# A decoder layer's output product: half of its weight sums made earlier and kept in DRAM

## The chip, the core and the metric

The kernel runs on one core of a Trainium2 chip. The metric is the device time of one execution in microseconds (us); the number that is predicted is the median of several runs.

## What is computed

One layer of a decoder over 512 tokens of width 2048, in float32: a norm, one combined projection `h @ w_in`, two groups of attention heads, the output product, and a gated feed-forward part. The change touches the output product alone:

```python
h = rms_norm(x, norm1_g[l])
proj = h @ w_in[l]
...
mix = jnp.concatenate([out_a.astype(x.dtype), out_b.astype(x.dtype)], axis=-1)
x = x + mix @ w_out[l]
h2 = rms_norm(x, norm2_g[l])
x = x + (jax.nn.silu(h2 @ w_gate[l]) * (h2 @ w_up[l])) @ w_down[l]
```

`w_out` is 2048 x 2048; its first half is its columns 0 to 1023.

## The kernel before

Every large product is cut into **pairs**: 1024 columns of a weight matrix, taken as two halves of 512 columns (`w1`, `w2`), against 512 rows of tokens. The reduction of 2048 is cut into four groups `g` of two 256-row halves. Within a group the 2 x 2 block product is done with seven products in place of eight (a Winograd form): three of them use a quarter of the weights as it is (`SINGLE`: P1 takes quarter a, P3 takes d, P2 takes c), four use a sum of quarters (`SUMS_OF`: P5 needs b - a, P6 needs d less that, P7 needs d - b, P4 needs c less the P6 sum). Seven products of four groups are 28 **items** of a pair, in the order P1 (items 0 to 3), P5 (4 to 7), P6 (8 to 11), P3 (12 to 15), P7 (16 to 19), P2 (20 to 23), P4 (24 to 27).

For an item `stream` (L318) issues four things. `total` (L325) calls `Pair.source`: the quarter is loaded with `load_quarter` (L219, DMA at L222, 512 KB, one tile of `wpool`, which has 12), and where a sum is due VectorE makes it in place at L256. `first_part` (L329) rounds the source to the high part `wh` on ScalarE (L331), `second_part` (L333) takes the low part `wl` on VectorE (L335). Then TensorE does 8 matmuls with `wh` and 4 with `wl` (L361). `wh` and `wl` have two tiles each, so an item can be prepared about two items ahead. TensorE, VectorE and ScalarE each take their instructions strictly in the order in which the scheduler put them, and so does the queue of SyncE (SP), which issues all loads and stores: a DMA that waits holds every DMA behind it.

Beside the items runs **background** work, one piece at a time after the `wh` matmuls of an item (`step`, L502): attention heads, transposes, and the activation side of the next product. `split` (L172) makes the high and low parts of an activation operand (ScalarE L174, VectorE L175).

The first pair (queries and keys of the gated heads) is issued by a table of its own (`first_pair`). `stream` does the others. In what follows they are counted as in the change: the **second pair** makes two value halves (`va1`, `va0`), the **third** `qb0`, `kb0`, the **fourth** `vb1`, `vb0`, the fifth `qb1`, `kb1`, the sixth the output gate. The **seventh** is the first half of the output product (`pair(opm, rows_mix, ocol(0), ocol(512), final_out(0), ...)`, L1416), the eighth its second half; eleven pairs of the gate and up products and six of the down product follow. In the seventh pair the background makes the operands S1, S2, S4, A12 and A22 of that same product (`late_jobs`, L1225: sums on VectorE at L1234, L1236, L1238 and a `split` each).

The second pair also carries `gates` (L768) and `bias_tables` (L598); the latter ends in `rep_d` (L618), one DMA of 2560 KB from DRAM to DRAM. The third and fourth carry the gated heads (`gla_head`, L823). `rpool` has four tiles of 128 x 512 floats; they hold activations in the first pair, and from the end of the fourth on the dilated heads and the sums of `late_jobs` use them. `final_proj` (L1084) stores each projection to DRAM (L1092).

## Time and profile before

| | |
|---|---|
| median of 3 runs | 1980.36 us (1979.09 to 1982.37) |
| the profiled execution, its own time | 1983.93 us |
| its span | 1982.1 us |
| TensorE busy | 1933.1 us (98%) |
| VectorE busy | 1652.7 us (83%) |
| ScalarE busy | 1095.9 us (55%) |
| GpSimd busy | 60.1 us (3%) |
| DMA moved | 360.44 MB, mean 182 GB/s |

The times in the trace are counted from the span's start. PE is TensorE's matmuls, PEld its weight loads, DVE is VectorE, ACT is ScalarE, POOL is GpSimd, and SPq is SyncE's queue, which issues the DMAs. An arrow in a group of instructions (`wl<-wa,wh`) reads "writes wl from wa and wh", with buffer numbers left out. The second pair stands from 105.0 to 184.1 us, the third to 277.3, the fourth to 363.5, and the seventh from 574.4 to 654.1. What ended an idle time stands behind `<-`. Busy times of PE are modelled, so the spacing of its starts says more than its durations.

### The profile page before, as it was taken

How to read it: one execution, taken by the hardware profiler on the slowest of the kernel's cores; microseconds unless marked ns; L12 is line 12 of the kernel's file. 1: busy time of each engine (PE TensorE's matmuls, PEld its weight loads, DVE VectorE, ACT ScalarE, POOL GpSimd, SP SyncE). 2: the span in 40 equal slices, each digit the busy share in tenths (PEclk: the TensorE clock that was granted, in tenths of full speed). 3: DMA queues.
4: the chain of work that ended last, by engine and by line, in shares of the span. 5: the costliest groups of instructions: out<-in, count | busy, mean ns of one | idle time of the engine just before them, and what ended most of it. 6: DMA issues, size and time to landing. Idle time of an engine off the chain costs nothing.

```text
span 1982.1 us, 25779 instructions
## 1 busy us (share of the span) xinstructions
PE 1933.1 (98%) x9226; PEld 1671.1 (84%) x9226; DVE 1652.7 (83%) x1850; ACT 1095.9 (55%) x1600; POOL 60.1 (3%) x81
## 2 busy tenths in 40 slices
PE   7999999999999999999999999999999999999998
PEld 6888888888787777888888888888888888888887
DVE  7997787768689789878878878878879989989987
ACT  6664564566676666545445445445446646546443
POOL 0000231011000000000000000000000000000000
PEclk9999999999999999999999999999999999999999
DMA  8357455454575685654554554554555855955762
GB/s 276 118 171 251 132 182 169 141 162 151 182 232 187 222 267 170 180 160 133 181 164 134 176 164 128 174 166 128 174 161 164 292 195 187 310 182 172 249 212 75
DMA packets 237113, 360.44 MB, mean 182 GB/s; under 512 B 18247, under 2 KB 96784, under 8 KB 236985
## 3 DMA queue, kind: packets, MB, share of 16 engines
q1 hardware_dynamic: 236776, 358.72, 57.1%
q8 instruction: 72, 1.18, 0.2%
q14 instruction: 57, 0.46, 0.1%
q10 hardware_dynamic: 208, 0.08, 0.0%
HBM read 296.59 MB, written 64.51 MB: 182 GB/s over the span
## 4 chain that ended last, share of the span: by engine, by line
PE 75%; DVE 8%; DMA 5%; issue 3%; ACT 2%; POOL 1%; SPq 0%; DVEq 0%; ACTq 0%; POOLq 0%
PE acc L361 70%; DVE wl L335 3%; DVE wa L256 2%; PE bank L1112 1%; DVE AS L175 1%; DMA xn_d<-PT 1%; PE bank L1009 1%; ACT wh L331 1%; PE bank L977 1%; DMA T<-x_d 0%; DMA top<-mix_d 0%; PE bank L1002 0%; DMA r<-xn_d 0%; DMA wc<-in_w_in 0%; DVE wb L256 0%
## 5 line engine op out<-in xcount | busy, mean ns | idle before, releaser
L361 PE MATMUL acc<-wh,AS 128*128 128x512 f32 x3008 | 712.7, 380 | 2.0 <-ACT wh L331 2.0
L361 PEld LDWEIGHTS acc<-wh,AS 128*128 128x128 f32 x3008 | 568.3, 189 | 84.8 <-ACT wh L331 4.0
L331 ACT CAST wh<-wa 128x1024 fp32r<-128x1024 f32 x376 | 393.3, 1048 | 401.3 <-PE acc L361 378.9
L361 PE MATMUL acc<-wh,AA 128*128 128x512 f32 x2256 | 537.1, 381 | 9.6 <-ACT wh L331 9.6
L335 DVE TENSOR_TENSOR wl<-wa,wh 128x1024 fp32r<-128x1024 f32 x376 | 456.9, 1219 | 85.0 <-ACT wh L331 49.6
L361 PEld LDWEIGHTS acc<-wh,AA 128*128 128x128 f32 x2256 | 427.4, 190 | 72.8 <-ACT wh L331 11.9
L361 PE MATMUL acc<-wl,AS 128*128 128x512 f32 x1504 | 396.6, 386 | 10.1 <-DVE wl L335 9.9
L361 PEld LDWEIGHTS acc<-wl,AS 128*128 128x128 f32 x1504 | 279.2, 189 | 64.0 <-DVE wl L335 23.1
L361 PE MATMUL acc<-wl,AA 128*128 128x512 f32 x1128 | 297.1, 386 | 2.8 <-DVE wl L335 2.7
L361 PEld LDWEIGHTS acc<-wl,AA 128*128 128x128 f32 x1128 | 210.5, 190 | 35.8 <-DVE wl L335 6.3
L331 ACT CAST wh<-wb 128x1024 fp32r<-128x1024 f32 x94 | 98.5, 1049 | 120.0 <-PE acc L361 112.9
L331 ACT CAST wh<-wc 128x1024 fp32r<-128x1024 f32 x94 | 98.3, 1047 | 112.9 <-PE acc L361 104.8
L331 ACT CAST wh<-wd 128x1024 fp32r<-128x1024 f32 x94 | 98.5, 1048 | 105.6 <-PE acc L361 101.5
L256 DVE TENSOR_TENSOR wa<-wc,wa 128x1024 f32<-128x1024 f32 x94 | 114.6, 1222 | 45.6 <-DMA wc<-in_w_gate 29.0
L335 DVE TENSOR_TENSOR wl<-wd,wh 128x1024 fp32r<-128x1024 f32 x94 | 114.4, 1220 | 38.5 <-ACT wh L331 29.5
L335 DVE TENSOR_TENSOR wl<-wc,wh 128x1024 fp32r<-128x1024 f32 x94 | 114.6, 1220 | 35.0 <-ACT wh L331 34.2
L335 DVE TENSOR_TENSOR wl<-wb,wh 128x1024 fp32r<-128x1024 f32 x94 | 113.6, 1217 | 4.9 <-ACT wh L331 4.4
L256 DVE TENSOR_TENSOR wb<-wd,wb 128x1024 f32<-128x1024 f32 x94 | 114.5, 1218 | 1.1 <-DMA wd<-in_w_in 0.7
L256 DVE TENSOR_TENSOR wa<-wb,wa 128x1024 f32<-128x1024 f32 x94 | 113.6, 1219 | 0.8
L256 DVE TENSOR_TENSOR wa<-wd,wa 128x1024 f32<-128x1024 f32 x94 | 112.8, 1218 | 0.1
L298 DVE SCALAR_TENSOR_TENSOR seed<-acc,rs,seed 128x512 f32<-128x512 f32 x96 | 70.4, 746 | 23.2 <-PE acc L361 23.2
L282 ACT ACTIVATE seed<-acc,rs 128x512 f32<-128x512 f32 x96 | 60.7, 682 | 1.2 <-PE acc L361 1.0
(289 smaller groups left out, 1368.7 us busy)
## 6 DMA issues: line engine op xcount, KB each, us to landing
wa<-in_w_gate SPq DMA_DIRECT2D x44, 512.0 KB, 4.2
wb<-in_w_up SPq DMA_DIRECT2D x44, 512.0 KB, 4.3
wd<-in_w_up SPq DMA_DIRECT2D x44, 512.0 KB, 4.4
wc<-in_w_gate SPq DMA_DIRECT2D x44, 512.0 KB, 3.7
wc<-in_w_in SPq DMA_DIRECT2D x28, 512.0 KB, 3.7
wa<-in_w_in SPq DMA_DIRECT2D x24, 512.0 KB, 5.1
wb<-in_w_in SPq DMA_DIRECT2D x24, 512.0 KB, 6.0
wd<-in_w_in SPq DMA_DIRECT2D x24, 512.0 KB, 5.4
```

Source lines behind the costliest of these rows:

```text
L175: nc.vector.tensor_tensor(a[:, :, 1, :], src, a[:, :, 0, :].bitcast(F32), op=ALU.subtract)
L256: nc.vector.tensor_tensor(src, self.quarter(one, g), src, op=ALU.subtract)
L282: nc.scalar.activation(halves(t), unfolded(src[m]), AF.Copy, scale=self.scale(half, m))
L298: nc.vector.scalar_tensor_tensor(halves(seed[m]), unfolded(src[m]), self.scale(half, m), halves(seed[m]), op0=ALU.mult, op1=ALU.add,)
L331: nc.scalar.copy(high[k], sources[k])
L335: nc.vector.tensor_tensor(low[k], sources.pop(k), high[k].bitcast(F32), op=ALU.subtract)
L361: nc.tensor.matmul(p.dst[prod][m], a[:, jj, hl, m * P : (m + 1) * P], folded(w[:, jj, :]), start=fresh and g == 0 and len(terms) == 2 and ...
L977: nc.tensor.matmul(lp[:, :n], qh[:, b * P : (b + 1) * P], kh[:, :n], start=True, stop=True)
L1009: nc.tensor.matmul(op, vh[:, k, :], lgs[b][:, k * P : (k + 1) * P], start=(k == 0), stop=(k == b))
L1112: nc.tensor.transpose(bk[:, jj, m * P : (m + 1) * P], tiles[m][:, f : f + P], ident)
```

## The change

The 16 sums of quarters that the seventh pair makes on VectorE are made elsewhere. A new generator `weight_sums` loads, for each group and each 128-row half of a quarter, the four quarters a, b, d, c of `w_out` into the four tiles of `rpool` (128 x 512, 256 KB each), makes the four sums there with four VectorE instructions, and stores each to a DRAM tensor (`P5_g_d`, `P7_g_d`, `P6_g_d`, `P4_g_d`). There are eight such rounds: 32 loads, 32 sums, 32 stores. `side(2)` takes one step of the generator at every second item of the second, third and fourth pair. In the seventh pair `source` loads a stored sum (512 KB) where it used to make it, and the quarters a, d and c are loaded for P1, P3 and P2 alone, and released after use; b is not loaded there any more.

```diff
         def source(self, prod, g):
             if prod in SINGLE:
-                return self.quarter(SINGLE[prod], g)
+                t = self.quarter(SINGLE[prod], g)
+                if self.sums:
+                    self.q.pop((SINGLE[prod], g))
+                return t
+            if self.sums:
+                t = wpool.tile([P, 2, 512], F32, name=nm("ws"), tag="w")
+                load(t, self.sums[prod, g])
+                return t
             one, two = SUMS_OF[prod]
...
+    def weight_sums(rows, w1, w2, sums):
+        tt = nc.vector.tensor_tensor
+        def fetch(g, j):
+            res = []
+            for name in "abdc":
+                r0 = rows[g][0 if name in "ab" else 1] + P * j
+                t = rpool.tile([P, 2, 256], F32, name=nm("r"), tag="r").rearrange(
+                    "p a b -> p (a b)")
+                load(t, (w1 if name in "ac" else w2)[r0 : r0 + P, :])
+                res.append(t)
+            return res
+        for g in range(4):
+            for j in range(2):
+                a, b, d, c = fetch(g, j)
+                yield
+                yield
+                tt(a, b, a, op=ALU.subtract)
+                tt(b, d, b, op=ALU.subtract)
+                yield
+                tt(d, d, a, op=ALU.subtract)
+                tt(c, c, d, op=ALU.subtract)
+                for prod, t in (("P5", a), ("P7", b), ("P6", d), ("P4", c)):
+                    store(sums[prod, g][:, j, :], t)
+                yield
...
+    def side(units):
+        count = [0]
+        def go():
+            count[0] += 1
+            if aside and count[0] % units == 0:
+                try:
+                    next(aside[0])
+                except StopIteration:
+                    aside.pop(0)
+        return go
+    def both(*fns):
+        return lambda: [fn() for fn in fns]
...
+    aside.append(weight_sums(rows_mix, ocol(0), ocol(512), out_sums))
+    beside = side(2)
-    pair(opx, rows_in, col(1536), col(1024), final_proj("va1", "va0"), rate((22, 1), (6, 0.6)),
+    pair(opx, rows_in, col(1536), col(1024), final_proj("va1", "va0"),
+         both(rate((22, 1), (6, 0.6)), beside),
          row_scale, before=lambda: background.extend([gates(), bias_tables()]))
     flow = rate((84, 0.55))
-    pair(opx, rows_in, col(3088), col(4112), final_proj("qb0", "kb0"), flow, row_scale)
-    pair(opx, rows_in, col(5648), col(5136), final_proj("vb1", "vb0"), flow, row_scale)
+    flowing = both(flow, beside)
+    pair(opx, rows_in, col(3088), col(4112), final_proj("qb0", "kb0"), flowing, row_scale)
+    pair(opx, rows_in, col(5648), col(5136), final_proj("vb1", "vb0"), flowing, row_scale)
...
-    pair(opm, rows_mix, ocol(0), ocol(512), final_out(0), paced([1] * 28),
+    pair(opm, rows_mix, ocol(0), ocol(512), final_out(0), paced([1] * 28), sums=out_sums,
```

The scheduler sets the order on each engine, and three places of it are shown. In the changed kernel line 335 of before is L371, line 256 is L264, line 1092 is L1146 and line 618 is L672; L345 to L349 are the new sums, L336 their loads, L351 their stores.

The first place is VectorE in the seventh pair, from the end of P5 into P6 (`wa<-wd,wa` are the sums for P6, `AS` the splits of S1, `r` the sums of `late_jobs`). Before:

```order
L1236 TENSOR_TENSOR r_5300<-r_5300,qT_5370 128x512
L256 TENSOR_TENSOR wa_5200<-wd_5463,wa_5200 128x1024
L175 TENSOR_TENSOR AS_1058_5454<-r_5300,AS_1058_5454 128x2x256
L335 TENSOR_TENSOR wl_5466<-wa_5314,wh_5461 128x1024
L1236 TENSOR_TENSOR r_5326<-r_5326,kT_5395 128x512
L256 TENSOR_TENSOR wa_5228<-wd_5488,wa_5228 128x1024
L175 TENSOR_TENSOR AS_1063_5479<-r_5326,AS_1063_5479 128x2x256
L335 TENSOR_TENSOR wl_5491<-wa_5200,wh_5486 128x1024
```

The same stretch with the change (`ws` is a stored sum):

```order
L371 TENSOR_TENSOR wl_5579<-ws_5551,wh_5575 128x1024
L175 TENSOR_TENSOR AS_1084_5568<-r_5470,AS_1084_5568 128x2x256
L175 TENSOR_TENSOR AS_1090_5594<-r_5444,AS_1090_5594 128x2x256
L1290 TENSOR_TENSOR r_5470<-r_5470,kT_5537 128x512
L371 TENSOR_TENSOR wl_5605<-ws_5577,wh_5601 128x1024
L175 TENSOR_TENSOR AS_1095_5618<-r_5470,AS_1095_5618 128x2x256
L1292 TENSOR_TENSOR r_5384<-v_5565,r_5384 128x512
L371 TENSOR_TENSOR wl_5629<-ws_5603,wh_5625 128x1024
```

The instruction of 1024 columns between two `wl` is gone, and more of the `late_jobs` work stands ahead of a given item.

The second place is SP's queue in the second pair, around `rep_d`; `wc` are the quarters for its P2 items, `va` the stores of a projection. Before, two of the four `wc` loads stand there:

```order
L222 DMA wc_1607<-in_w_in 128x2x512
L618 DMA rep_d<-bias_d 1024x1x640
L1092 DMA va_177<-seed_1471 128x512
L1092 DMA va_177<-seed_1489 128x512
L222 DMA wc_1626<-in_w_in 128x2x512
```

With the change:

```order
L351 DMA P_0_d<-r_1458 128x512
L672 DMA rep_d<-bias_d 1024x1x640
L351 DMA P_0_d<-r_1460 128x512
L1146 DMA va_177<-seed_1511 128x512
L1146 DMA va_177<-seed_1529 128x512
L336 DMA r_1613<-in_w_out 128x512
L336 DMA r_1615<-in_w_out 128x512
L336 DMA r_1617<-in_w_out 128x512
L222 DMA wc_1663<-in_w_in 128x2x512
L222 DMA wc_1682<-in_w_in 128x2x512
```

The third and fourth `wc` loads now stand behind `rep_d`, two stores of a projection and three loads into `r` tiles, whose last one needs the tile of the store just behind `rep_d`.

The third place is VectorE in the P2 items of the second pair (items 20 to 23). Before:

```order
L335 TENSOR_TENSOR wl_1609<-wc_1587,wh_1605 128x1024
L298 SCALAR_TENSOR_TENSOR seed_1410<-acc_1147,rs_103,seed_1410 128x512
L335 TENSOR_TENSOR wl_1628<-wc_1607,wh_1624 128x1024
L256 TENSOR_TENSOR wa_1187<-wc_1626,wa_1187 128x1024
L335 TENSOR_TENSOR wl_1659<-wc_1626,wh_1656 128x1024
```

With the change:

```order
L371 TENSOR_TENSOR wl_1665<-wc_1643,wh_1661 128x1024
L306 SCALAR_TENSOR_TENSOR seed_1442<-acc_1163,rs_103,seed_1442 128x512
L345 TENSOR_TENSOR r_1611<-r_1613,r_1611 128x512
L346 TENSOR_TENSOR r_1613<-r_1615,r_1613 128x512
L348 TENSOR_TENSOR r_1615<-r_1615,r_1611 128x512
L349 TENSOR_TENSOR r_1617<-r_1617,r_1615 128x512
L264 TENSOR_TENSOR wa_1166<-wc_1663,wa_1166 128x1024
L371 TENSOR_TENSOR wl_1684<-wc_1663,wh_1680 128x1024
```

A whole round of four new sums and one sum of the pair itself stand between the second and the third `wl` of P2. In the whole order 16 of the 32 new sums stand ahead of the third pair's first `wl` and 16 in the third pair; none is left for the fourth.

## Rows read from the trace of the kernel before

**Rows 1.** The page, part 1: busy us (share of the span) xinstructions of each engine.

```profile
PE 1933.1 (98%) x9226; PEld 1671.1 (84%) x9226; DVE 1652.7 (83%) x1850; ACT 1095.9 (55%) x1600; POOL 60.1 (3%) x81
```

**Rows 2.** The page, part 4: the chain that ended last, by engine.

```profile
PE 75%; DVE 8%; DMA 5%; issue 3%; ACT 2%; POOL 1%; SPq 0%; DVEq 0%; ACTq 0%; POOLq 0%
```

**Rows 3.** Busy time of each engine in stretches; the first line names the columns.

```profile
core 0: us, PE busy (x) PEld busy (x) DVE busy (x) ACT busy (x) POOL busy (x), PEclk, DMA share, GB/s
105.00:184.00 79.00, 77.85 (x363) 66.28 (x362) 66.57 (x70) 41.29 (x51) 0.39 (x2) 1.00 0.61 202
184.00:277.30 93.30, 93.01 (x474) 79.92 (x473) 73.67 (x96) 50.21 (x111) 17.03 (x27) 1.00 0.58 178
574.40:654.10 79.70, 76.21 (x354) 64.52 (x353) 78.39 (x91) 51.16 (x76) 0.00 (x0) 1.00 0.60 198
900.00:975.00 75.00, 74.38 (x353) 64.83 (x352) 60.10 (x59) 36.95 (x43) 0.00 (x0) 1.00 0.51 158
165.00:184.00 19.00, 19.00 (x96) 16.44 (x95) 12.72 (x16) 8.30 (x10) 0.39 (x2) 1.00 0.87 283
```

**Rows 4.** L361, seventh pair: what TensorE sat idle for: us, times.

```profile
  DVE wl L335: 8.5, 10
```

**Rows 5.** Timeline of PE, seventh pair: starts of the wh matmuls of single items.

```profile
592.21 1.89 PE L361 MATMUL acc<-wh,AS 128*128 128x512 f32 x8
...
609.43 1.89 PE L361 MATMUL acc<-wh,AS 128*128 128x512 f32 x8
...
612.02 1.89 PE L361 MATMUL acc<-wh,AS 128*128 128x512 f32 x8
...
614.62 1.89 PE L361 MATMUL acc<-wh,AS 128*128 128x512 f32 x8
...
630.15 1.89 PE L361 MATMUL acc<-wh,AS 128*128 128x512 f32 x8
...
633.33 1.89 PE L361 MATMUL acc<-wh,AA 128*128 128x512 f32 x8
```

**Rows 6.** Timeline of DVE, seventh pair: one item's instructions: start us, us.

```profile
597.91 0.68 DVE L1236 TENSOR_TENSOR r<-r,kT 128x512 f32<-128x512 f32 x1
598.51 1.22 DVE L256 TENSOR_TENSOR wa<-wd,wa 128x1024 f32<-128x1024 f32 x1
599.65 0.68 DVE L175 TENSOR_TENSOR AS<-r,AS 128x512 fp32r<-128x512 f32 x1
600.25 1.22 DVE L335 TENSOR_TENSOR wl<-wa,wh 128x1024 fp32r<-128x1024 f32 x1
601.38 0.68 DVE L1238 TENSOR_TENSOR r<-v,r 128x512 f32<-128x512 f32 x1
```

**Rows 7.** L361, second and third pair: what TensorE sat idle for: us, times.

```profile
  DVE wl L335: 4.1, 6
```

**Rows 8.** Timeline of SP's DMA issues, second pair: start us, us.

```profile
145.55 0.72 SPq L618 DMA_DIRECT2D rep_d<-bias_d  x1
151.79 2.11 SPq L1092 DMA_DIRECT2D va<-seed  x2
153.95 0.43 SPq L222 DMA_DIRECT2D wc<-in_w_in  x1
...
165.16 1.49 SPq L222 DMA_DIRECT2D wa<-in_w_in  x3
```

**Rows 9.** DMA issues of the second pair: xcount, KB each, median us to landing.

```profile
wc<-in_w_in SPq DMA_DIRECT2D x4, 512.0 KB, 3.6
...
wb<-in_w_in SPq DMA_DIRECT2D x4, 512.0 KB, 7.5
va<-seed SPq DMA_DIRECT2D x6, 256.0 KB, 9.5
```

**Rows 10.** Timelines of ACT and PE, second pair, item 22: its cast and its first matmuls.

```profile
162.70 1.05 ACT L331 CAST wh<-wc 128x1024 fp32r<-128x1024 f32 x1 [1.54 <-PE acc L361]
...
165.96 1.89 PE L361 MATMUL acc<-wh,AA 128*128 128x512 f32 x8
```

11 lines of the change are left out of this document (8 added, 3 removed).

## The prediction

> **What bounds the kernel now.** First the busy shares, then the chain that ended last. TensorE is busy for 98% of the span, with VectorE next at 83% [rows 1], and the chain stands 75% on TensorE and 8% on VectorE [rows 2]. So a change can win only where TensorE waits, and it loses where it makes TensorE wait. Third, the stretches [rows 3]: a quiet pair of the feed-forward part takes 75.0 us with 60.1 us of VectorE work. The seventh pair takes 79.7 us with 78.4 us of VectorE work: there VectorE is full. Fourth, what TensorE waits for there: VectorE's `wl`, ten times, 8.5 us with matmuls and weight loads counted both [rows 4]. The starts of the items give the loss without double counting. An undisturbed item takes 614.62 - 612.02 = 2.60 us. The five from 592.21 to 609.43 take 17.22 us where 5 x 2.60 = 13.0 us would do, and the one from 630.15 to 633.33 takes 3.18 us [rows 5]. That is 4.2 + 0.6 = 4.8 us. The comparison with the quiet pair gives 79.7 - 75.0 = 4.7 us [rows 3]. Fifth, VectorE inside one slow item [rows 6]: sum, weight sum, split and `wl` start at 597.91, 598.51, 599.65 and 600.25, and the next item's first at 601.38, so one item costs VectorE 3.47 us. Its two sizes cost 0.60 us (512 columns) and 1.14 us (1024), start to start.
>
> **What is removed.** The seventh pair loses 16 weight sums, 16 x 1.14 = 18.2 us of VectorE [rows 6]. Without its weight sum the slow item needs 3.47 - 1.14 = 2.33 us, under the 2.60 us of TensorE. More work of the background comes into some items in its place (first place in the order: two splits and a sum before one `wl`, 3 x 0.60 + 1.14 = 2.94 us), but others get lighter, and `wl` can be two items ahead. So I take the whole 4.8 us as gained. Bounds: half of it (2.4 us), if the background's own loads now hold VectorE; 5.5 us, if also waits on ScalarE in that pair shrink.
>
> **What is added, VectorE.** 32 sums of 512 columns, 32 x 0.60 = 19.2 us, 16 in the second and 16 in the third pair: 9.6 us each. They are covered by VectorE's idle time there, 79.0 - 66.6 = 12.4 us and 93.3 - 73.7 = 19.6 us [rows 3]. The cover is not even. Where four new sums stand together before one `wl` (third place in the order), that item needs 0.67 (a `seed`, taken a little over the 512-column sum) + 4 x 0.60 + 2 x 1.14 = 5.4 us against 2.6 us, and the lead of two items just about pays for it. I take 0.5 us for such places. Bounds: 2 us, and a gain of 1 us, since TensorE already waits 4.1 us for `wl` in these two pairs [rows 7] and the new order also moves work out of some of those waits.
> [...] The rows have two starts of 0.60 us in place of one of 1.14 us [rows 6], 16 x 0.06 = 1 us in all, and I go by the rows.
>
> **What is added, DMA in the second and third pair.** 32 loads and 32 stores of 256 KB, 16.8 MB, half of it in each pair. The second pair moved 202 GB/s at a share of 0.61, which is 331 GB/s at full share; with 8.4 MB over 79 us it would move 308 GB/s [rows 3]. Its last 19 us are at 283 GB/s and a share of 0.87 already [rows 3]. So transfers queue there, and what counts is who stands behind whom on SP. The worst place I find is the second place in the order. The third `wc` quarter now stands behind a load into an `r` tile that must wait for the store just behind `rep_d` to land. `rep_d` was issued at 145.55 and the first store after it at 151.79 [rows 8]; such stores took 9.5 us to land [rows 9]. So that tile comes free at about 161, the `wc` load goes out at about 162 and lands 3.6 us later at best [rows 9], at 165.6. Its cast ran at 162.70 with TensorE's item at 165.96 [rows 10]; the latest harmless start is 165.96 - 1.05 = 164.9. So it is 0.7 us late at best, and 4.6 us if it takes the 7.5 us that the `wb` loads took [rows 9]. Three loads leave just ahead of it, so I take 1.5 us, nearer to the 3.6 us row because those loads are small. Lower bound 0.
> Other waits that are added cost nothing by their leads. New stores that wait on SP for a VectorE sum hold the third pair's `wa` loads, which went out from 165.16 on [rows 8] and are first needed near 183, 18 us later. `gates`, `rep_d` and the heads shift by one or two VectorE instructions and are read a pair later. GpSimd's queue is not touched.
>
> **What is added, DMA in the seventh pair.** 28 loads of 512 KB where there were 16: 6.3 MB more over 79.7 us, 79 GB/s on top of 198 at a share of 0.60 [rows 3], so some 0.84. Each weight tile is now used by one item and free again, so the twelve tiles run further ahead of TensorE than before. I cost this at nothing; if that cover fails it is the 2.4 us of the lower bound above.
>
> **Sum.** -4.8 + 0.5 + 1.5 = -2.8 us against the profiled execution's own 1983.93 us, that is 1981.1 us. That execution lies 3.6 us above the median of the runs, so in terms of the median 1980.36 - 2.8 = 1977.6 us. About 0.2%, 4 us, is what a measurement of this kernel can tell from no change.
>
> **The rivals.**
> *Clean gain.* The loads find room, the late `wc` quarter is no later than its slack, and the crowded places fall into existing waits: -4.8 to -5.5 us, 1975.3 us. For it: VectorE has 32 us idle in the two pairs [rows 3]. Against it: the SP order above.
> [...]
> *Half a gain.* In the seventh pair the loads of `late_jobs` stand on SP between loads of weights, each of which now waits for an item's `wl`. If they come late, splits hold the casts and 2.4 us are left of the gain: -2.4 + 2.0 = -0.4 us, 1980.0 us. Against it: `late_jobs` fetches three pieces ahead.
> *Slower: SP's queue in the second and third pair.* The wait of a load for a store decides, from the point where a store takes the 9.5 us of the `va` row [rows 9] everywhere and not only behind `rep_d`. Then the `wc` quarter is 4.6 us late. The third pair's `wa` quarters, behind four stores that wait for sums near 168 and four loads that wait for these to land, go out at about 180 where they went at 165.16 [rows 8], land 7.5 us later [rows 9] and hold the pair's start by some 4 us (187.5 against a need near 183). With 0.5 us for crowding: 4.6 + 4 + 0.5 - 4.8 = +4.3 us, 1984.7 us. For it: 0.87 of the DMA engines busy at that place [rows 3]. Against it: the `wc` loads landed in 3.6 us.
>
> **How the numbers follow.** Forecast 42%, clean gain 25%, half a gain 15%, slower 18%. Faster by over 0.2%: the clean gain and the lowest part of the forecast, 0.30. Slower by over 0.2%: the last rival and a little of the half gain, 0.20. Within 0.2%: 0.50. The range goes from the clean gain with the repeat spread of 1.3 us below the median (1974.0) to the slow rival's value with a little over it (1985.5); the forecast's own range, 1976 to 1980, is the sum with the `wc` term between 0 and 3 us.
>
> **What would show it.** Right: in the seventh pair VectorE's busy time falls by some 18 us, TensorE's waits for `wl` fall from 8.5 to under 2 us, and the pair takes about 75 us; in the second pair a cast of `wc` waits for its DMA by one to two us near item 22, and TensorE after it; the third pair is as long as before. Wrong: if the seventh pair stays over 77 us, its limit was not the weight sums; if the second and third pair together grow by over 5 us, or TensorE waits for `wa` at the third pair's start, the SP term was too small; if they do not grow at all, it was imagined.

## The result, and the profile after

Six runs of the changed kernel have a median of 1988.03 us (1985.34 to 1997.26), six of the kernel before 1980.57 us (1979.09 to 1982.37). The ratio is 1.0034 with an interval of 1.0020 to 1.0048: the change costs 4 to 9.5 us. The prediction of 1977.6 us was wrong, and so was its range, which ended at 1985.5 us.

The two profiled executions show less than that. The one of before took 1983.93 us, above all its timed runs; the one of after took 1985.34 us, the lowest of its six. So the traces tell where time went, and the runs tell how much. Busy time first (page, part 1, kernel after):

```profile
PE 1931.9 (97%) x9226; PEld 1670.8 (84%) x9226; DVE 1654.8 (83%) x1866; ACT 1095.4 (55%) x1600; POOL 67.6 (3%) x81
```

Against [rows 1] nothing of note moved: VectorE has 2.1 us more work in all, and the totals hide two changes that nearly cancel. The stretches show them. These are the second, third and seventh pair of after (columns as in [rows 3]):

```profile
105.00:191.00 86.00, 80.68 (x363) 67.76 (x363) 75.68 (x86) 41.27 (x51) 0.45 (x2) 0.96 0.74 236
191.00:290.60 99.60, 94.37 (x476) 79.83 (x475) 84.01 (x112) 50.61 (x112) 22.87 (x27) 1.00 0.88 283
...
584.60:660.90 76.30, 74.80 (x354) 65.08 (x353) 62.69 (x76) 50.77 (x76) 0.00 (x0) 1.00 0.92 302
```

The seventh pair is 3.4 us shorter, with 15.7 us less of VectorE's work [rows 3]; TensorE's waits for `wl`, 8.5 us in [rows 4], are gone, and this is all that is left there (what L397's matmuls and weight loads sat idle for, after, seventh pair):

```profile
  ACT wh L367: 3.3, 2
```

But the second pair is 7.0 us longer and the third 6.0 us. Lengths of pairs are taken here and below from the first `wh` matmul of a pair to that of the next. All else is 8.2 us shorter by these two traces, 3.6 us of it in the sixth pair and 4.8 us in the eighth. The sixth pair takes 109.6 to 114.2 us in the kernels of this study, whatever was changed elsewhere, so its part can't be told from chance. Of the eighth pair's 4.8 us, 3.3 us stand at its items 1 to 4 and belong to the gain: in 15 of the 17 kernels whose seventh pair makes none or half of its sums these items are 2.7 to 3.3 us shorter than before (in hole 1.2 us shorter, in skip_second 0.5 us longer), and in cost_alone, which makes them all, 0.3 us longer. Its last item takes from 2.2 us less to 0.8 us more in these kernels without any pattern, so its 1.4 us are not told from chance either.

**The second pair.** SP's queue (after, timeline of its issues; start us, us):

```profile
145.87 0.72 SPq L672 DMA_DIRECT2D rep_d<-bias_d  x1
148.30 3.38 SPq L351 DMA_DIRECT2D P_d<-r  x1
152.37 2.11 SPq L1146 DMA_DIRECT2D va<-seed  x2
154.53 8.65 SPq L336 DMA_DIRECT2D r<-in_w_out  x3
163.22 0.94 SPq L222 DMA_DIRECT2D wc<-in_w_in  x2
...
181.29 2.06 SPq L222 DMA_DIRECT2D wa<-in_w_in  x4
```

A store of a sum leaves just behind `rep_d`. Three loads into `r` tiles follow at 154.53, and their issue takes 8.65 us: the last waits for that store to land. The two `wc` quarters stand behind it and go out at 163.22; before, the later of them went at 153.95 [rows 8]. In the second and third pair such waits add up to this (after, waits of SP's queue: us, times, longest):

```profile
SPq L336 <- DMA P_d<-r: 17.2, 11, 7.3
```

ScalarE's cast for item 22 and TensorE's matmuls of items 21 to 23 show what it costs (after, timelines of ACT and PE; compare [rows 10]):

```profile
169.71 1.04 ACT L367 CAST wh<-wc 128x1024 fp32r<-128x1024 f32 x1 [8.41 <-DMA wc<-in_w_in]
```

```profile
165.22 1.03 PE L397 MATMUL acc<-wl,AA 128*128 128x512 f32 x4
170.81 3.78 PE L397 MATMUL acc<-wh,AA 128*128 128x512 f32 x8 [4.55 <-ACT wh L367]
174.38 1.55 PE L397 MATMUL acc<-wl,AA 128*128 128x512 f32 x4
175.77 1.89 PE L397 MATMUL acc<-wh,AA 128*128 128x512 f32 x8
```

TensorE waits 4.55 us for item 22. Then it needs 4.96 us (170.81 to 175.77) for it, where an undisturbed item takes 2.59 us: 3.78 us for eight matmuls where 1.89 us stands below. The granted clock says why (after, stretches):

```profile
165.00:170.00 5.00, 1.25 (x6) 0.76 (x4) 2.97 (x5) 0.29 (x1) 0.00 (x0) 0.86 0.94 288
170.00:175.00 5.00, 4.20 (x10) 3.39 (x11) 4.28 (x4) 2.17 (x3) 0.00 (x0) 0.50 1.00 361
175.00:180.00 5.00, 5.00 (x24) 4.35 (x23) 2.88 (x3) 1.72 (x2) 0.00 (x0) 0.96 0.54 164
```

After a stretch in which TensorE worked 1.25 us of 5 it gets 0.50 of its clock; the stretch from 175 us is back at 0.96. So the late quarter costs 4.7 us of waiting and 2.4 us of slow matmuls. The second part does not follow every wait: in cost_alone TensorE waits 3.63 us at the same place, the clock stays at 1.00, and the next eight matmuls take 1.99 us.

**The third pair.** No single long wait stands there. TensorE waits for VectorE's `wl` (after, third pair; 1.0 us in the same pair before):

```profile
  DVE wl L371: 10.6, 7
```

By the starts of its items, against before, the 6.0 us stand at item 7 (2.1 us) and at items 16, 18 and 19 (0.3, 1.8 and 1.9 us). VectorE in turn waits for quarters of weights (after, third pair, waits), and has less idle time to catch up in: it works 84.0 of 99.6 us, where before it worked 73.7 of 93.3 us [rows 3].

```profile
DVE wa L264 <- DMA wc<-in_w_in: 3.6, 2, 3.0
...
DVE wa L264 <- DMA wb<-in_w_in: 3.3, 3, 1.8
```

From the timelines of DVE and PE (after, third pair): a weight sum waits 3.05 us for its quarter, and from there to 256 us VectorE has hardly any idle time (one wait of 0.57 us). The `wl` of item 7 starts at 217.43, that of item 19 at 261.18.

```profile
216.64 0.88 DVE L977 SCALAR_TENSOR_TENSOR oT<-bank,so,gb 128x256 f32<-128x256 f32 x2 [0.88 <-POOL so L159]
217.43 1.22 DVE L371 TENSOR_TENSOR wl<-wa,wh 128x1024 fp32r<-128x1024 f32 x1
...
238.95 1.23 DVE L264 TENSOR_TENSOR wa<-wc,wa 128x1024 f32<-128x1024 f32 x1 [3.05 <-DMA wc<-in_w_in]
...
253.92 0.68 DVE L348 TENSOR_TENSOR r<-r,r 128x512 f32<-128x512 f32 x1
254.63 0.69 DVE L349 TENSOR_TENSOR r<-r,r 128x512 f32<-128x512 f32 x1
255.24 1.22 DVE L371 TENSOR_TENSOR wl<-wb,wh 128x1024 fp32r<-128x1024 f32 x1
...
258.70 0.69 DVE L1118 TENSOR_TENSOR seed<-seed,ss 128x512 f32<-128x512 f32 x1 [0.49 <-POOL ss L159]
260.57 0.69 DVE L1118 TENSOR_TENSOR seed<-seed,ss 128x512 f32<-128x512 f32 x1 [1.18 <-POOL ss L159]
261.18 1.22 DVE L371 TENSOR_TENSOR wl<-wb,wh 128x1024 fp32r<-128x1024 f32 x1
```

```profile
218.70 1.13 PE L397 MATMUL acc<-wl,AS 128*128 128x512 f32 x4 [1.80 <-DVE wl L371]
...
262.45 1.13 PE L397 MATMUL acc<-wl,AS 128*128 128x512 f32 x4 [2.08 <-DVE wl L371]
```

These two `wl` stand behind other work that waits for GpSimd: an `oT` of the heads (0.88 us), and two `seed` instructions (0.49 and 1.18 us). Before, item 19's `wl` had only one of those `seed`s between it and the `wl` ahead of it (before, timeline of DVE), and the `wl` of item 7 stood ahead of the `oT`.

```profile
244.16 1.22 DVE L335 TENSOR_TENSOR wl<-wb,wh 128x1024 fp32r<-128x1024 f32 x1
...
247.33 0.69 DVE L1064 TENSOR_TENSOR seed<-seed,ss 128x512 f32<-128x512 f32 x1 [0.49 <-POOL ss L159]
247.94 1.22 DVE L335 TENSOR_TENSOR wl<-wb,wh 128x1024 fp32r<-128x1024 f32 x1
```

So the scheduler's order on VectorE changed in this pair too.

### The profile page after: what moved, and what is told of

It is laid out like the page before. It is cut to its first block, busy times and chain, and to the rows that moved or that the text cites. A ratio compares the mean times of both kernels' runs of the same rounds, so it can differ in the third digit from the quotient of the medians.

```text
span 1983.5 us, 25924 instructions
## 1 busy us (share of the span) xinstructions
PE 1931.9 (97%) x9226; PEld 1670.8 (84%) x9226; DVE 1654.8 (83%) x1866; ACT 1095.4 (55%) x1600; POOL 67.6 (3%) x81
## 3 DMA queue, kind: packets, MB, share of 16 engines
q8 instruction: 72, 1.18, 0.3%
## 4 chain that ended last, share of the span: by engine, by line
PE 72%; DVE 7%; DMA 4%; issue 2%; ACT 1%; SPq 0%; POOL 0%; DVEq 0%; ACTq 0%
PE acc L397 68%; DVE wl L371 3%; PE bank L1166 1%; DVE wa L264 1%; DMA k<-y_d 1%; PE bank L1063 1%; PE bank L1031 1%; ACT wh L367 1%; DVE AS L175 1%; DMA xn_d<-oT 1%; PE bank L1056 0%; DMA T<-p_d 0%; DVE wb L264 0%; DMA q<-y_d 0%; DVE seed L1379 0%
## 5 line engine op out<-in xcount | busy, mean ns | idle before, releaser
L397 PE MATMUL acc<-wh,AS 128*128 128x512 f32 x3008 | 713.1, 380 | 2.5 <-ACT wh L367 2.5
L397 PEld LDWEIGHTS acc<-wh,AS 128*128 128x128 f32 x3008 | 568.7, 189 | 84.8 <-ACT wh L367 3.9
L367 ACT CAST wh<-wa 128x1024 fp32r<-128x1024 f32 x364 | 381.1, 1048 | 400.4 <-PE acc L397 368.4
L397 PE MATMUL acc<-wh,AA 128*128 128x512 f32 x2256 | 537.1, 381 | 12.9 <-ACT wh L367 12.9
L371 DVE TENSOR_TENSOR wl<-wa,wh 128x1024 fp32r<-128x1024 f32 x364 | 442.5, 1219 | 82.4 <-ACT wh L367 47.2
L397 PEld LDWEIGHTS acc<-wh,AA 128*128 128x128 f32 x2256 | 427.7, 190 | 76.5 <-ACT wh L367 15.3
L397 PE MATMUL acc<-wl,AS 128*128 128x512 f32 x1504 | 395.2, 385 | 9.0 <-DVE wl L371 8.7
L397 PEld LDWEIGHTS acc<-wl,AS 128*128 128x128 f32 x1504 | 279.0, 189 | 61.8 <-DVE wl L371 20.9
L397 PE MATMUL acc<-wl,AA 128*128 128x512 f32 x1128 | 296.6, 385 | 2.7 <-DVE wl L371 2.7
L397 PEld LDWEIGHTS acc<-wl,AA 128*128 128x128 f32 x1128 | 210.1, 190 | 35.8 <-DVE wl L371 6.2
L367 ACT CAST wh<-wc 128x1024 fp32r<-128x1024 f32 x94 | 98.3, 1047 | 120.7 <-PE acc L397 101.4
L367 ACT CAST wh<-wb 128x1024 fp32r<-128x1024 f32 x90 | 94.3, 1049 | 121.4 <-PE acc L397 110.7
L371 DVE TENSOR_TENSOR wl<-wc,wh 128x1024 fp32r<-128x1024 f32 x94 | 114.6, 1221 | 38.9 <-ACT wh L367 38.0
L371 DVE TENSOR_TENSOR wl<-wd,wh 128x1024 fp32r<-128x1024 f32 x94 | 114.6, 1220 | 37.6 <-ACT wh L367 28.7
L264 DVE TENSOR_TENSOR wa<-wc,wa 128x1024 f32<-128x1024 f32 x90 | 109.8, 1222 | 41.0 <-DMA wc<-in_w_gate 26.5
L264 DVE TENSOR_TENSOR wa<-wb,wa 128x1024 f32<-128x1024 f32 x90 | 108.6, 1219 | 4.0 <-DMA wb<-in_w_in 3.3
L371 DVE TENSOR_TENSOR wl<-wb,wh 128x1024 fp32r<-128x1024 f32 x90 | 108.7, 1218 | 3.3 <-ACT wh L367 3.3
L264 DVE TENSOR_TENSOR wb<-wd,wb 128x1024 f32<-128x1024 f32 x90 | 109.6, 1219 | 0.4
L264 DVE TENSOR_TENSOR wa<-wd,wa 128x1024 f32<-128x1024 f32 x90 | 108.1, 1218 | 0.1
L306 DVE SCALAR_TENSOR_TENSOR seed<-acc,rs,seed 128x512 f32<-128x512 f32 x96 | 70.3, 746 | 22.8 <-PE acc L397 22.8
```

What stands on the lines that cost most here:

```text
L264: nc.vector.tensor_tensor(src, self.quarter(one, g), src, op=ALU.subtract)
L306: nc.vector.scalar_tensor_tensor(halves(seed[m]), unfolded(src[m]), self.scale(half, m), halves(seed[m]), op0=ALU.mult, op1=ALU.add,)
L367: nc.scalar.copy(high[k], sources[k])
L371: nc.vector.tensor_tensor(low[k], sources.pop(k), high[k].bitcast(F32), op=ALU.subtract)
L397: nc.tensor.matmul(p.dst[prod][m], a[:, jj, hl, m * P : (m + 1) * P], folded(w[:, jj, :]), start=fresh and g == 0 and len(terms) == 2 and ...
```

## The experiments

The first theory was that SP's queue and the transfers make the loss; the rivals were VectorE's 19 us of sums, and the 16.8 MB as such. All ratios are to the kernel before, run on the same chip in the same session (its medians there: 1981.9 to 1983.6 us, and 1980.6 us beside the change, which was not run again beside the others); the difference is worked out from the ratio with 1982 us. Pair lengths are from one profiled execution each, intervals are of the runs.

| kernel | ratio (95%) | us | 2nd | 3rd | 4th | 7th pair |
|---|---|---|---|---|---|---|
| before | 1 | 0 | 79.1 | 93.2 | 86.1 | 79.6 |
| the change | 1.0034 (1.0020 to 1.0048) | +6.7 | 86.1 | 99.2 | 86.3 | 76.3 |
| gain_alone | 0.9972 (0.9960 to 0.9984) | -5.5 | 79.9 | 93.6 | 86.3 | 78.0 |
| cost_alone | 1.0062 (1.0046 to 1.0078) | +12.3 | 82.9 | 101.4 | 86.2 | 80.6 |
| dma_only | 1.0005 (0.9996 to 1.0015) | +1.0 | 84.3 | 93.2 | 86.2 | 80.0 |
| vector_only | 1.0035 (1.0017 to 1.0052) | +6.9 | 92.4 | 93.7 | 86.2 | 77.1 |
| vector_paced | 0.9968 (0.9954 to 0.9981) | -6.3 | 79.4 | 93.2 | 86.6 | 77.0 |
| pool_paced | 1.0073 (1.0055 to 1.0092) | +14.5 | 84.7 | 97.8 | 92.1 | 77.1 |
| no_store | 1.0013 (1.0002 to 1.0025) | +2.6 | 81.2 | 101.4 | 86.1 | 79.4 |
| late_stores | 1.0033 (1.0016 to 1.0051) | +6.5 | 85.7 | 101.9 | 86.9 | 76.5 |
| skip_second | 1.0024 (1.0007 to 1.0041) | +4.8 | 79.1 | 98.3 | 89.8 | 77.5 |
| pool_sums | 1.0175 (1.0154 to 1.0196) | +34.7 | 98.3 | 109.0 | 86.2 | 77.7 |
| half_late | 0.9976 (0.9962 to 0.9989) | -4.8 | 79.1 | 94.6 | 88.5 | 75.9 |
| half_later | 0.9998 (0.9985 to 1.0010) | -0.4 | 79.1 | 94.8 | 90.7 | 76.9 |
| both_untied | 1.0047 (1.0031 to 1.0063) | +9.3 | 88.8 | 96.2 | 86.2 | 80.5 |
| hole | 1.0061 (1.0046 to 1.0076) | +12.1 | 87.7 | 92.9 | 92.8 | 79.2 |
| half_spread | 1.0022 (1.0005 to 1.0039) | +4.4 | 81.7 | 98.6 | 87.7 | 75.7 |
| drop_four | 1.0021 (1.0011 to 1.0030) | +4.2 | 80.6 | 99.7 | 86.0 | 77.2 |
| no_load | 0.9999 (0.9984 to 1.0013) | -0.2 | 81.3 | 95.5 | 86.7 | 77.3 |

### Gain and cost apart

**gain_alone**, no sums made, plain quarters loaded in their place:

```diff
-                load(t, self.sums[prod, g])
-                return t
+                two = SUMS_OF[prod][1]
+                return load_quarter(self.rows, two, g, self.w1 if two in "ac" else self.w2)
...
-    aside.append(weight_sums(rows_mix, ocol(0), ocol(512), out_sums))
```

> The sums are not made at all; the seventh pair loads sixteen plain quarters of the output weight in their place (its products are therefore of other weights), so this is the change's gain without its cost. Theory (the gain is there, the loss lies in the second and third pair): the seventh pair takes 75 to 76.5 us where it took 79.6, the second and third pair stay at 79 and 93 us, and the whole is 4 to 6 us under the kernel before. Rival (the gain is not there, since the seventh pair was bound by something else): within 2 us of the kernel before.

**cost_alone**, the sums made and not read:

```diff
-    pair(opm, rows_mix, ocol(0), ocol(512), final_out(0), paced([1] * 28), sums=out_sums,
+    pair(opm, rows_mix, ocol(0), ocol(512), final_out(0), paced([1] * 28),
```

> The sums are made and stored as in the change, but the seventh pair makes its own as before and never reads them, so this is the change's cost without its gain. Theory: the second pair takes 85 to 87 us and the third 98 to 100 us, together 11 to 14 us more, and the whole is 10 to 14 us over the kernel before. Rival (the two traces read so far differ mostly by chance, and the loss lies elsewhere): under 5 us over the kernel before.

Measured: -5.5 us for the gain and +12.3 us for the cost, and their sum, +6.8, is the change's +6.7. So the gain is real and as large as forecast, and the loss lies in the making. cost_alone's second and third pair together grow by 12.0 us, as expected, but not each as expected (82.9 and 101.4 us). The gain lies in two pairs: the seventh of gain_alone takes 78.0 us, over the 75 to 76.5 expected, and the eighth 85.3 us against 89.2. In the seventh VectorE waits are down to 1.0 us, but ScalarE is late twice (what the stream's matmuls and weight loads sat idle for there):

```profile
  ACT wh L366: 5.2, 2
  DVE wl L370: 1.0, 2
```

### The cost in two parts

**dma_only**, pieces loaded and stored without a sum:

```diff
-                tt(a, b, a, op=ALU.subtract)
-                tt(b, d, b, op=ALU.subtract)
                 yield
-                tt(d, d, a, op=ALU.subtract)
-                tt(c, c, d, op=ALU.subtract)
```

> The change without its 32 sums: the pieces of the output weight are loaded into the r tiles and stored again unsummed, in the same places of the order, and the seventh pair reads them (so it multiplies by plain weights). Theory (the loss is SP's queue and the transfers): within 2.5 us of the changed kernel, 5 to 9 us over the kernel before; the second pair stays near 86 us. Rival (the loss is the 19 us of sums that crowd VectorE): 3 to 6 us under the kernel before, as with the gain alone.

**vector_only**, sums of a constant, no transfers:

```diff
-                load(t, (w1 if name in "ac" else w2)[r0 : r0 + P, :])
...
-                tt(a, b, a, op=ALU.subtract)
+                tt(a, m, m, op=ALU.subtract)
...
-                    store(sums[prod, g][:, j, :], t)
```

> The change's 32 sums on VectorE in the same places of the order, but of a constant that lies in SBUF, with no load and no store; the seventh pair loads plain quarters of the output weight (its products are of other weights). Theory (SP's queue): 2 to 6 us under the kernel before, at most 2 us slower than the gain alone. Rival (VectorE crowding): 4 to 8 us over the kernel before, near the changed kernel, with the third pair at 96 us or more and TensorE waiting for wl there.

**vector_paced**, the same with the newest `wl` as the constant:

```diff
+                m = newest[0][:, 0, :].bitcast(F32)
+                tt(a, m, m, op=ALU.subtract)
+                tt(b, m, m, op=ALU.subtract)
```

> The run before this with the sums on VectorE alone had 20 of its 32 sums one behind the other (nothing held them back), so it did not tell. Here each sum reads the newest wl tile, so that it cannot run ahead of its place: 32 sums of 128x512 spread over the two pairs, no load and no store of them, the seventh pair on plain quarters of the output weight. Theory (SP's queue makes the loss: stores wait there for sums, loads for stores, and weight quarters stand behind both): second pair 79 to 80.5 us, third 93 to 94.5 us, the whole 3 to 6 us under the kernel before. Rival (19 us more of VectorE crowd the two pairs): third pair 96 us or more, the whole from 1 us under to 6 us over the kernel before.

vector_only missed the theory, and of the rival it met the whole (+6.9 us) but not the third pair (93.7 us). Nothing held its sums back, and the scheduler, which fixes each engine's order when the kernel is built, put 20 of the 32 one behind the other; from the timeline of DVE there:

```profile
164.23 0.67 DVE L348 TENSOR_TENSOR r<-mats 128x512 f32<-128x512 f32 x1
164.83 0.67 DVE L344 TENSOR_TENSOR r<-mats 128x512 f32<-128x512 f32 x1
```

A `wl` came 10 us late behind them. That is a fault of the experiment, and vector_paced mends it: with the sums in their places VectorE carries 8 us more in the third pair and loses nothing, and the whole is 6.3 us under the kernel before, no worse than the gain alone. The rival "VectorE's time alone" falls. The transfers alone cost 6.5 us over the gain (1.0 + 5.5), most of it in the second pair (84.3 us against gain_alone's 79.9) and some in the seventh (80.0 against 78.0): half of what was expected of them, and between the two theories. In the second pair it is not the change's loss: by the starts of its items 2.1 us stand at item 2 and 2.2 us at item 12, where TensorE waits for a small load, and none at the `wc` quarters. The third pair is untouched. The third pairs of dma_only and of vector_paced:

```profile
189.30:282.50 93.20, 92.91 (x473) 79.81 (x472) 73.75 (x96) 50.09 (x112) 17.77 (x27) 1.00 0.78 245
```

```profile
182.60:275.90 93.30, 93.00 (x474) 80.00 (x474) 81.65 (x111) 50.16 (x112) 18.08 (x27) 1.00 0.58 177
```

So 245 GB/s cost the third pair nothing, the 16 sums in it cost it nothing, and yet the change loses 6 us there. (The bytes are not quite the change's: 245 GB/s over 93.2 us are 22.8 MB, and the change moves 28.2 MB in its third pair.) The first theory does not explain that.

### Queues, stores and pacing

**pool_paced**, the sums' transfers on GpSimd's queue (with a copy of one column that paces each piece):

```diff
-                load(t, (w1 if name in "ac" else w2)[r0 : r0 + P, :])
+                if name == "a":
+                    nc.vector.tensor_copy(t[:, :1], newest[0][:, 0, :1].bitcast(F32))
+                nc.gpsimd.dma_start(t, (w1 if name in "ac" else w2)[r0 : r0 + P, :])
...
-                    store(sums[prod, g][:, j, :], t)
+                    nc.gpsimd.dma_start(sums[prod, g][:, j, :], t)
```

> The whole change, but the loads and stores of the sums go through GpSimd's queue, so that nothing of them stands on SP; a copy of one column paces each piece's first load. The sums on VectorE and the 16.8 MB stay. Theory (SP's queue): second pair 79 to 82 us, third 93 to 95 us, the whole 1 to 5 us under the kernel before. Rival (VectorE crowding, or the bytes themselves): the two pairs together stay 9 us or more over the kernel before, the whole 3 to 8 us over it.

**no_store**, loads and sums without stores:

```diff
-                for prod, t in (("P5", a), ("P7", b), ("P6", d), ("P4", c)):
-                    store(sums[prod, g][:, j, :], t)
```

> The sums are loaded and made in the places of the change but not stored; the seventh pair loads plain quarters of the output weight (its products are of other weights). So no load waits for a store to land and no store waits on SP for a sum. Theory (SP held by stores): 2 to 5 us under the kernel before, third pair under 95 us. Rival (VectorE crowding): third pair 97 us or more, the whole within 2 us of the kernel before or over it.

**late_stores**, wider pacing on SP:

```diff
                 a, b, d, c = fetch(g, j)
                 yield
                 yield
+                yield
+                yield
...
-    beside = side(2)
+    beside = side(1)
```

(and one more step ahead of the stores, three behind them)

> The whole change on SP's queue, paced otherwise: of each piece the loads, five items later the first sums, two items later the four stores and four items later the next piece's loads, spread over three pairs in place of two and a quarter; so a store finds its sum made and a load its tile free. Theory (SP's queue): from 4 us under to 1 us over the kernel before, SP's waits of a load for a store to land under 5 us in the second to fourth pair where they are 17.2 us. Rival (VectorE crowding or the bytes): 4 us or more over the kernel before.

In all three the theory's numbers missed and the rival's came, but for pool_paced's whole (+14.5 us where the rival said 3 to 8), though vector_paced rules out the rival's reason. pool_paced is the slowest: leaving SP does not help, and since it also moved heads and held GpSimd with 56 issues of some 0.55 us each in the two pairs, it doesn't tell the theories apart. late_stores did not reach its pacing: SP's waits of a load for a store are still 16.5 us; it seems that the steps of the generator set only a priority and that the scheduler issues a load as soon as it believes that its tile is free. From here on a load was held back by a copy of one column from the newest `wl`. no_store is the telling one. It moves fewer bytes than dma_only and no store waits for anything, and its third pair is the longer by 8 us (third pair of no_store, and what the stream's matmuls and weight loads sat idle for there):

```profile
185.00:286.30 101.30, 95.84 (x473) 80.59 (x472) 83.80 (x112) 50.29 (x111) 19.55 (x27) 0.98 0.68 213
```

```profile
  DVE wl L368: 11.6, 9
```

The bytes don't do it: they are 21.6 MB there, less than in dma_only. What no_store has and neither dma_only nor vector_paced has is VectorE instructions that need a piece to have landed, and loads on SP that wait for a sum to leave their tile (9.9 us in its third pair, the longest 8.7 us). New theory: two causes. In the second pair, `wc` quarters stand on SP behind loads that wait for stores. In the third, VectorE, whose instructions run in the scheduler's order (in the change a weight sum that waits 3.05 us holds the work behind it), is tied to the pieces' loads while it has no room left.

### Another place, another engine, half the sums

**skip_second**, nothing before the third pair:

```diff
-         both(rate((22, 1), (6, 0.6)), beside),
+         rate((22, 1), (6, 0.6)),
```

> All 32 sums as in the change, but none before the third pair: 16 in the third and 16 in the fourth (a copy of one column holds each piece's first load back to its place), so the second pair with rep_d and its late wc quarters is left alone. Theory (two causes: in the second pair weight quarters on SP stand behind loads of pieces; in the third VectorE waits in its order for late transfers while it has no room left): second pair 79 to 80 us, third 96 to 100 us, fourth 86 to 88 us, the whole from 2 us under to 3 us over the kernel before. Rival (the 16.8 MB cost the same wherever they go): the second to fourth pair together 11 us or more over the kernel before, the whole 4 to 8 us over it.

**pool_sums**, the sums on GpSimd:

```diff
-        tt = nc.vector.tensor_tensor
+        tt = nc.gpsimd.tensor_tensor
```

> The change with its 32 sums on GpSimd in place of VectorE; loads and stores on SP's queue as in the change. Theory: the third pair loses its stalls, as VectorE neither waits for pieces nor has the sums to do (93 to 95.5 us), the second keeps the late wc quarter (83 to 87 us), the whole within 3 us of the kernel before. Rival (the third pair's stalls come from late weight quarters alone): third pair 97 us or more and the whole 4 us or more over the kernel before.

**half_late** and **half_later**, P5 and P6 alone, from the third pair on, the second of them begun at its item 18 with a step at every item:

```diff
-            if self.sums:
+            if self.sums and prod in ("P5", "P6"):
...
-                a, b, d, c = fetch(g, j)
+                a, b, d = fetch(g, j)
...
-                for prod, t in (("P5", a), ("P7", b), ("P6", d), ("P4", c)):
+                for prod, t in (("P5", a), ("P6", d)):
```

> Only the sums of P5 and P6, which the seventh pair needs where its stalls lie (items 2 to 10); P7 and P4 are summed there as before. 16 sums, 24 loads and 16 stores in place of 32, 32 and 32, one half in the third and one in the fourth pair. Theory: second pair 79 to 80 us, third 94 to 97 us, fourth 86 to 88 us, seventh 75.5 to 77.5 us, the whole 1 to 5 us under the kernel before. Rival (bytes cost wherever they are): the two pairs together 5 us or more over the kernel before, and no gain.

> The same half, pushed further: from item 21 of the third pair to item 15 of the fourth, so that the part of the third pair that stalled in the change is left alone. Theory: second pair 79 to 80, third 93 to 95, fourth 86 to 89, seventh 75.5 to 77.5 us, the whole 2 to 5 us under the kernel before, and so faster than both kernels. Rival (16 sums within 22 items crowd VectorE, or the bytes cost there too): third and fourth together 4 us or more over the kernel before, no gain.

skip_second bears out the second pair: 79.1 us, as before. The third (98.3 us) still loses, and now the fourth too, more than expected of it: 8.7 us together, below the rival's 11, while the whole, +4.8 us, lies in the rival's range. pool_sums missed the theory by far; the rival's numbers came, but the run can't bear it out, since GpSimd was itself too slow. GpSimd needs 1.26 to 4.59 us for a sum that takes VectorE 0.69 us, and VectorE itself slows down meanwhile, to 1369 ns for a `wl` that takes 1218 ns in the change (DVE groups, second and third pair of pool_sums; then the first of GpSimd's):

```profile
L371 DVE TENSOR_TENSOR wl<-wa,wh 128x1024 fp32r<-128x1024 f32 x32 | 43.4, 1369 | 5.6 <-PE acc L397 2.7 <-ACT wh L367 2.7
```

```profile
L345 POOL TENSOR_TENSOR r<-r,r x7: 1263/1612/4592, 130.8 to 261.9; 128x512 f32<-128x512 f32 x7
```

What makes VectorE's instructions longer there is not shown by any run.

half_late is the version that beats both kernels: 4.8 us under the kernel before (2.2 to 7.5), some 11 us under the change. It moves the eight sums of items 4 to 11, near which the stalls of the seventh pair lay, and leaves the other eight where they were. All came as expected but for the fourth pair, half a us over. Its third, fourth and seventh pair:

```profile
183.70:278.30 94.60, 93.18 (x473) 79.75 (x472) 78.73 (x110) 50.09 (x111) 18.82 (x27) 1.00 0.73 238
278.30:366.80 88.50, 86.27 (x419) 73.32 (x418) 69.89 (x89) 43.20 (x75) 14.04 (x15) 1.00 0.69 218
574.90:650.80 75.90, 75.69 (x353) 64.62 (x352) 71.06 (x84) 50.36 (x76) 0.00 (x0) 1.00 0.83 270
```

The seventh pair is 3.7 us shorter with 71 us of VectorE's work left in it: it was full at 78.4 us [rows 3], and a small relief is enough. half_later, the same 16 sums of 512 columns in 22 items, gives 6.2 us away in the third and fourth pair and gains nothing that can be measured: there its rival was right.

### The two causes by themselves

**both_untied**, transfers as in dma_only and VectorE's time beside them, untied:

```diff
-                tt(a, b, a, op=ALU.subtract)
-                tt(b, d, b, op=ALU.subtract)
+                m = newest[0][:, 0, :].bitcast(F32)
+                busy(m)
+                busy(m)
...
+            nc.vector.tensor_reduce(idle, m, axis=mybir.AxisListType.X, op=ALU.add)
```

> The change's loads and stores of pieces, unsummed, as in the run with transfers alone, and beside them 32 VectorE instructions of 512 columns (sums along the row of the newest wl) in the places of the sums: the transfers and VectorE's time together, but VectorE never waits for a piece and no store for VectorE (the seventh pair multiplies by plain weights). Theory (the third pair stalls since VectorE, full there, waits in its order for pieces and late quarters): second pair 82 to 86 us as with the transfers alone, third pair 93 to 95.5 us, the whole from 1 us under to 3 us over the kernel before. Rival (transfers and VectorE's time together are enough, tied or not): third pair 97 us or more, the whole 5 to 9 us over it.

**hole**, no piece near `rep_d`:

```diff
-            if aside and count[0] % units == 0:
+            if aside and count[0] % units == 0 and not 8 < count[0] < 26:
```

> All 32 sums as in the change, begun in the second pair, but none of their loads goes out between items 8 and 26 of it, where rep_d and the last wc quarters stand on SP (a copy of one column holds every piece's load back); they end in the fourth pair. Theory (the second pair's loss is the wc quarters behind loads that wait for stores behind rep_d): second pair 79 to 80.5 us with two pieces' sums still in it, third 96 to 99, fourth 88 to 91 us, the whole 1 to 5 us over the kernel before. Rival (any sums or transfers in the second pair cost there): second pair 82 us or more.

**half_spread**, half_late with that hole, begun in the second pair, and a wider step:

```diff
-    beside = side(2)
+    beside = side(2.5)
```

> Only the sums of P5 and P6, spread wider: one piece in the first eight items of the second pair, none in the rest of it, the others in the third and fourth pair at five items for two steps. Theory (sums and transfers cost only where VectorE or SP has no room): second pair 79 to 80.5, third 93.5 to 95, fourth 87 to 89, seventh 75.5 to 77 us, the whole 4 to 7 us under the kernel before and so under the changed kernel by over 10 us. Rival (half the sums give half the gain, and the rest is chance): within 2 us of the kernel before.

**drop_four**, the change without the stores just behind `rep_d`:

```diff
-                    store(sums[prod, g][:, j, :], t)
+                    if (g, j) != (0, 1):
+                        store(sums[prod, g][:, j, :], t)
```

> The change without four of its 32 stores: those of the second piece, which stand right behind rep_d on SP. All other instructions keep their order on SP and VectorE but for neighbours; the seventh pair loads plain quarters of the output weight (its products are of other weights). Theory (loads of the third piece wait on SP for these stores to land, and the third and fourth wc quarter behind them): wc quarters issued by 157 us where they went at 163.2, second pair 79 to 81 us, third 97 to 100 us as in the change, the whole 4 to 7 us under the changed kernel, so from 1 us under to 3 us over the kernel before. Rival (the second pair's loss comes from the bytes, or from another load): second pair 83 us or more.

**no_load**, sums of the newest `wl` into the `r` tiles, stored, nothing loaded:

```diff
-                load(t, (w1 if name in "ac" else w2)[r0 : r0 + P, :])
...
-                tt(a, b, a, op=ALU.subtract)
+                m = newest[0][:, 0, :].bitcast(F32)
+                tt(a, m, m, op=ALU.subtract)
```

> The change's 32 sums and 32 stores without its 32 loads: each sum reads the newest wl, so VectorE waits for no piece, but stores wait on SP for sums as in the change (the seventh pair loads plain quarters of the output weight; its products are of other weights). Theory (third pair: VectorE, full, waits in its order for pieces): third pair 93 to 95 us, the whole from 5 us under to 1 us over the kernel before. Rival (third pair: SP's stores that wait for sums make the weight quarters late): third pair 97 us or more, the whole 2 us or more over it.

drop_four shows the second pair's cause in its trace. With four stores gone and the order kept but for one load, which now stands ahead of `rep_d`, the loads no longer wait, and the quarters go out 7.3 us earlier (its SP queue):

```profile
145.71 0.72 SPq L672 DMA_DIRECT2D rep_d<-bias_d  x1
153.93 0.98 SPq L1146 DMA_DIRECT2D va<-seed  x2
154.96 0.95 SPq L335 DMA_DIRECT2D r<-in_w_out  x2
155.96 1.78 SPq L222 DMA_DIRECT2D wc<-in_w_in  x2
```

The pair takes 80.6 us with the sums still in it, item 22 is 1.7 us late in place of 4.7, and no slow item follows (the pair's clock is 1.00, where the change's is 0.96); the third pair stays at 99.7 us. The runs don't confirm the size: the whole is +4.2 us, over the 3 us expected at most, so the gain over the change is 0.13% or 2.6 us, where 4 to 7 us were expected, and the two intervals overlap.

hole and half_spread, both past the second pair's 80.5 us, told nothing of the quarters, since holding the pieces back moved a head. Its products came one behind the other at the end of the second pair, and TensorE had no item to do from 183.3 to 193.2 us (hole, timeline of PE):

```profile
188.46 0.29 PE L940 MATMUL bank<-qT,kT 128*64 128x128 f32 x1 [2.84 <-DVE qT L926]
```

half_spread, which was to be the best, is 9 us worse than half_late, and the moved head does not explain all of it: its third pair takes 98.6 us with only about eight sums in it. both_untied has another order again, with 88.8 us in the second pair: there SP's stores wait 21.6 us for their loads, a small load of a one-hot matrix stands behind one, and TensorE waits for it; with the slow matmuls behind that wait this is 7 of the pair's 9.7 us:

```profile
147.83 1.34 PE L674 MATMUL bank<-v,T 33*8 33x512 f32 x2 [3.74 <-DMA v<-in_onehot]
```

It is a wait behind a wait on SP once more, with another victim.

For the third pair the two runs come out between the theories; no_load's whole, -0.2 us, is the theory's, both_untied's, +9.3 us, is just over the rival's, by its second pair. Untied, transfers and VectorE's time together make it 96.2 us; with stores that wait for sums but no loads (no_load) it is 95.5 us. The third pairs of both_untied and no_load:

```profile
194.80:291.00 96.20, 93.17 (x473) 79.73 (x472) 82.30 (x112) 50.09 (x112) 20.07 (x27) 1.00 0.76 237
```

```profile
185.60:281.20 95.60, 93.53 (x474) 79.71 (x474) 82.57 (x111) 50.20 (x112) 20.07 (x27) 1.00 0.71 224
```

All five kernels with the 32 sums tied to loads on SP's queue, begun in the second pair, have 99.2 to 101.9 us there (the change, cost_alone, no_store, late_stores, drop_four; hole is left out, since its third pair lost the head to the second); the four without the tie have 93.2 to 96.2 (dma_only, vector_paced, both_untied, no_load). So of the 6 us some 2 to 3 come with sums and transfers that meet in one pair, and the larger part with the tie.

What the tie does is not shown, and the traces name a rival for it: the scheduler's order on VectorE, which changes with the tie. The second `seed` wait of 1.18 us ahead of item 19's `wl` stands in the five tied kernels, in half_spread and in pool_sums. The first six of these lose 3.3 to 6.1 us at items 18 to 20; of the kernels without it none loses over 1.5 us there but skip_second and pool_paced (5.0 and 5.2 us). half_spread has it with half the sums, and half_late, with half the sums and without it, takes 94.6 us. both_untied loses the change's 2.1 us at item 7, with the change's `oT` ahead of the `wl`, and 0.9 us at item 19. In the tied kernels up to four sums stand between two `wl`, in the untied ones two. VectorE's own waits for pieces can't be all of it: the change has none of note in its third pair, only the 6.9 us for weight quarters. SP's waits for sums alone are not enough: no_load's stores wait 14.4 us for them in its third pair, and it loses 2.3 us. A kernel with tied sums in the order of the untied ones was not tried.

## Why the prediction was wrong

**The gain was right.** "So I take the whole 4.8 us as gained": gain_alone measures 5.5 us (3.2 to 7.9). VectorE's waits went as said, and its busy time in the pair fell by 15.7 us (18 was said). By the starts of the items the stalls at items 2 to 10 and 19 shrink by 5.1 us, but the pair by 3.4 us only, and 3.3 us more are gained in the eighth, which the prediction did not name; so the sum of the gain came near partly by luck. The seventh takes 76.3 us and not 75, since a piece of the "half a gain" rival is in it. ScalarE waits 1.8 us for a load of `late_jobs` (`kT`, issued at 612.49, its cast at 618.37), and item 12 is 1.6 us late. "I cost this at nothing" was too little for the transfers there, by 1.6 us; in the other kernels that make no sums there, items 12 and 13 lose 1.9 to 4.8 us.

**VectorE's crowding was right by itself.** 0.5 us taken, nothing measurable in vector_paced. The price of 0.60 us for a 512-column sum held too: the starts of the row of sums in vector_only are 0.60 us apart. Each of these sums is 0.67 us long, and the next one starts before its end.

**The `wc` term had the right place and the wrong size.** "Three loads leave just ahead of it, so I take 1.5 us, nearer to the 3.6 us row because those loads are small." The load went out at 163.2 us, 1 us later than worked out. Its cast started 6.5 us after the issue, so the row to take was the 7.5 us one. The bound of 4.6 us from that row nearly met the delay of item 22 (4.7 us). What no bound had was the clock: it stood at half when the item ran, 2.4 us more. In sum 7.1 us against 1.5. The transfers at full share then, 361 GB/s in the stretch from 170 us, were above the 331 GB/s worked out from the rows, and single slices of 0.6 us of this trace reached 416 GB/s.

**The step that failed outright was the third pair.** "Other waits that are added cost nothing by their leads. New stores that wait on SP for a VectorE sum hold the third pair's `wa` loads [...] first needed near 183, 18 us later." The `wa` loads went out from 181.29, not 165.16; the lead of 18 us was spent. The pair's start was not held by them; later in it VectorE's weight sums waited 6.9 us for `wb` and `wc` quarters. The idle VectorE time, "19.6 us", was counted as cover for the sums and at the same time as room for waits, from the totals alone: neither late transfers nor the order of VectorE in this pair, where `wl` now stands behind instructions that wait for GpSimd, had a term. In the sum the third pair stood at nothing beyond the 0.5 us for crowding, and it cost 6.0 us by the trace. Which part is the late transfers and which the order stays open.

**The slow rival** had the mechanism of the second pair and the issue time of `wa` (about 180) right, and was given 18%. Its total of 1984.7 us was low by the clock and by the third pair, and the range ended with it. The sign for being wrong was named ("if the second and third pair together grow by over 5 us"): they grew by 13.0 us.

## What to carry to other kernels

Work that is moved to an idle stretch of an engine must be priced with its transfers and with everything that stands behind them in the issuing queue: here a load into a tile that a store had to leave first held the loads behind it on SP's queue for 7.3 us, until that store had landed. Idle time of an engine whose order is fixed is cover once only, either for added work or for late data: the 19.6 us of VectorE in the third pair were counted for both. Where a scheduler sets the order, read the new order of such an engine wherever work was added, and look for what a critical instruction now stands behind. And move only as much as the full stretch needs to be relieved of: half of the sums here brought most of the gain in half_late, though half_spread, with the same sums at other places, lost it again.

## What was not expected of the hardware

A wait of 4.55 us on TensorE cost a further 2.4 us, because the granted clock stood at 0.50 for the next item, where a wait of 3.63 us in cost_alone left it at 1.00; in the prediction every wait had been priced at its own length. Sums on GpSimd did not run beside VectorE for free: VectorE's instructions took up to a third longer as means of a group (`wa<-wd` 1618 ns against 1219), and the kernel lost 35 us. And the spread of the runs is part of a change's cost: the kernel with 20 sums in a row ran between 1981 and 1998 us, half_late between 1973 and 1982.
